# Layer 0's entry: six tiles of the first head summed side by side, between the modulation quarters

## The chip, the cores and the metric

One core of a Trainium2 chip runs the whole kernel. The metric is the device time of one execution in microseconds, here the median of several runs. In the profile PE is the matrix engine (PEld its weight loads), DVE, ACT and POOL are the vector, scalar and general-purpose engines, and SP issues most DMAs.

## What is computed

Two layers of a transformer over 512 latent tokens and 256 context tokens, D = 1024, in float32. Each layer is a mixer followed by a gated feed-forward, and each of the two reads a normalised input that is scaled and shifted by vectors made from a conditioning vector:

```python
s_c = jax.nn.silu(c)                       # (1, 1024); s_cc the same for the context
mx = (s_c @ mod_w[l] + mod_b[l])[:, None]  # 6 x 1024 numbers: shift, scale, gate, twice
shx1, scx1, gx1, shx2, scx2, gx2 = jnp.split(mx, 6, axis=-1)
hx = _rms(x, norm_mix_w[l]) * (1.0 + scx1) + shx1
qa_x, ka_x, va_x, qb_x, kb_x, vb_x = heads(hx @ w_in, True)    # layer 0
```

The change concerns only the beginning of layer 0: the first two of the six modulation parts (shift `part` 0 and scale `part` 1), the normalised and modulated input, and its product with the columns of `w_in` that belong to the first of four KV heads (256 query columns, 64 key, 64 value: 384 columns).

## The kernel before

**Tiles.** The 768 tokens are six tiles of 128: 0 to 3 latent, 4 and 5 context. `CTX_FIRST = (4, 5, 0, 1, 2, 3)` is the order in which they are worked. D is eight K-slices of 128 (`KT`). A product in float32 is done as three products of `float32r` halves: every operand is split into a high half (a cast on ACT) and a low half (a subtraction on DVE or POOL), and `project` (L460) adds high x high, high x low and low x high for each K-slice. So a tile's sum for one head is 8 x 3 = 24 products of 128 x 384.

**Modulation.** `mod_steps` (L168) makes a quarter `n` (256 columns, two K-slices of the later input) of one `part`: two loads of 512 KB (`modw`, L177), products with the padded conditioning columns (L182), a copy to SBUF (`modr`, L185), then `yield`; after it, four small products that turn the row into columns (`modcol`, L191) and `add_mod` (L276, L280), which writes the shift `modc` or the scale `aff`. The `modw` tiles and the head's weight tiles share the tag `mw` with six buffers; two more stand under the tag `raw`.

**The entry, L1149 to L1213.** Quarters 0 and 1 are started, the x tiles loaded; each x tile is squared (ACT, L1166), scaled by its inverse root (POOL L159 and L160, DVE L1167), transposed on PE (L1171) and copied to `xT` on ACT (L1172). Then quarter 2, and quarter 3 under a PE order that is written out by hand (`manual_schedule`); elsewhere a list scheduler orders each engine's instructions ahead of time, by program order and its own cost model. `modulated(k)` applies scale and shift to K-slice k of `xT` (DVE, L1184), casts the high halves (ACT, L1189) and subtracts for the low ones (L1190: POOL for the context's two tiles, DVE for the latent tiles). `weights0` (L481) loads the head's weights in four units of two K-slices (`wir`, L491) and splits them (L498, L499). The hand-written part sums only the two context tiles, and that in pieces around the end of quarter 3; their PSUM banks are halves of `inps` tiles of the score pool.

**Behind it.** `tables0` makes the rotary tables (`rw`, `rp`, `rt`, L383 to L392). `in_proj0` (L505) goes through the tiles in `CTX_FIRST` order: for each it sums what is not yet summed (`project`, in four quarters between which it yields), copies the sum out of PSUM (`qkv`, L520, two buffers), squares and reduces (L440, L442), takes the inverse root on POOL (L159, L160), rotates (`qy`, `qz`, L449 to L457, two buffers each), scales (L523) and splits into high and low halves for queries (`qd`) and keys (`kd`, the low half on POOL at L530). PE turns them (`qpt`, `kpt`) and ACT copies them out (`qt`, `kT`); with both context tiles' `kT` the first scores can start (L578). The sums of tiles 2 and 3 stand in the banks `acc0` and `acc1`. All sums of the later heads use `acc0`, so head 1 starts when tile 2 has been copied out. From then on each attention step of one head carries a tile's sums of the next.

Of the kernel before, what the change touches and what calls it, by code (L numbers as in the profile page):

```python
# [11 lines left out]
F32 = mybir.dt.float32  # L12
# [21 lines left out]
THETA = 10000.0  # L34
CTX_FIRST = (4, 5, 0, 1, 2, 3)
WBUF = 5
PBUF = 4
MODS0 = (0, 2, 2, 0)
LAM_INIT = 0.8 - 0.6 * math.exp(-0.3)
# [24 lines left out]
def backbone(es: ExitStack, tc: tile.TileContext, x, c, ctx, c_ctx, mod_w, mod_b, norm_mix_w, norm_ffn_w,  # L64
# [103 lines left out]
    def mod_steps(l, part, n, new_tile, pool, bank, wide=None, room=("modr", 1)):  # L168

        width, pieces = 256, 2  # L170
        c0 = part * D + n * width
        ps = p_1.tile([P, width], F32, name="mod", tag=bank) if wide is None else \
            wide.pool.tile([P, 1024], F32, name="mod", tag="sc", bufs=2)[:, :width]
        kp = KT // pieces
        for pc in range(pieces):
            w = new_tile([P, kp, width], "modw")
            nc.sync.dma_start(  # L177
                w, mod_w[l, pc * kp * P:(pc + 1) * kp * P, c0:c0 + width].rearrange("(j p) n -> p j n", p=P))
            for a in range(kp):
                k = pc * kp + a  # L180
                j = k % 4
                nc.tensor.matmul(ps[32 * j:32 * j + 32, :], s_pad[:, k, :], w[:, a, :],  # L182
                                 start=k < 4, stop=k >= 4, tile_position=(0, 32 * j))
        r = pool.tile([P, width], F32, name="modr", tag=room[0], bufs=room[1])
        turn["modr"] = nc.scalar.copy(r, ps)  # L185
        yield
        nb = width // P
        k0, k1 = n * nb, (n + 1) * nb
        pc2 = p_1.tile([P, nb, 2], F32, name="modcol", tag=bank)
        for b in range(nb):  # L190
            nc.tensor.matmul(pc2[:, b, :], r[:, b * P:(b + 1) * P], sel2, start=True, stop=True)  # L191
        add_mod(l, part, k0, k1, pc2, 2)
# [285 lines left out]
        return hi, lo  # L478


    def weights0(b, wp, subs, new_tile=raw_tile, loads=((0, 1), (), (2,), (3,))):  # L481

        qc, kc, vc = ((b * 256, 512 + 64 * b, 640 + 64 * b) if b < 2 else
                      (768 + (b - 2) * 256, 1280 + 64 * (b - 2), 1408 + 64 * (b - 2)))
        for u in range(4):
            if not u:
                raws = []
            for v in loads[u]:
                raws.append(new_tile([P, 2, 384], "wir"))
                for c0, c1, s in ((0, 256, qc), (256, 320, kc), (320, 384, vc)):  # L490
                    turn["load"] = nc.sync.dma_start(  # L491
                        raws[-1][:, :, c0:c1],
                        ev_w_in[0, v * 256:(v + 1) * 256, s:s + c1 - c0].rearrange("(j p) n -> p j n", p=P))
            if not u:
                yield
            raw = raws.pop(0)
            hi, lo = (wp.tile([P, 2, 384], F32R, name=f"wi{z}", tag=f"w{z}", bufs=WBUF + 1) for z in ("hi", "lo"))
            nc.scalar.copy(hi, raw)  # L498
            subs[u % len(subs)].tensor_sub(lo, raw, f32(hi))  # L499
            yield hi, lo  # L500
# [4 lines left out]
    def in_proj0(b, ws, tabs, wp, st, later, begun={}):  # L505
# [5 lines left out]
        for t in CTX_FIRST:  # L511
            ps = begun[t] if t in begun else acc_tile("inps", 384, one=int(b == 0 and t == CTX_FIRST[-1]))
            for k in range(0, KT, 2):
                if k:
                    yield
                if b == 0 and t in CTX_FIRST[:2]:
                    continue
                project(ps, t, ws, 0, 384, range(k, k + 2))
            raw = wp.tile([P, 384], F32, name="qkv", tag="qkv", bufs=2)
            nc.scalar.copy(raw, ps)  # L520
            nc.gpsimd.tensor_copy(vv[:, t, :], raw[:, 320:384])
            y, r = rotate(raw[:, 0:320], 4, 1, t, *tabs[b // 2], wp)
            nc.gpsimd.tensor_tensor(y, y, bc(r, 2, HD), ALU.mult)  # L523
            qd = wp.tile([P, 4, 2, HD], F32R, name="qd", tag="qd", bufs=2)
            nc.scalar.copy(qd[:, :, 0, :], y[:, 0:4])
            nc.vector.tensor_sub(qd[:, :, 1, :], y[:, 0:4], f32(qd[:, :, 0, :]))
            kd = wp.tile([P, 2, 2, HD], F32R, name="kd", tag="kd", bufs=2)
            kb = bc(y[:, 4, :], 1, 2)
            nc.scalar.copy(kd[:, 0], kb)
            nc.gpsimd.tensor_sub(kd[:, 1], kb, f32(kd[:, 0]))  # L530
# [616 lines left out]


    def start_tile(shape, name):  # L1149
        return start.pool.tile(shape, F32, name=name, tag="mw", bufs=6)  # L1150

    def start_mod(n):
        for part in range(2):
            mod_chunk(0, part, n, start_tile, start.pool, f"acc{part}", p_sc)

    p_sc = Pool("p_sc0", space=PSUM)
    wp = Pool("mw0", "right")
    xs = {t: load_x(t) for t in CTX_FIRST[:2]}
    start_mod(0)
    start_mod(1)  # L1160
    xs.update({t: load_x(t) for t in CTX_FIRST[2:]})
    xT = start.pool.tile([P, KT, TOK], F32, name="xT")
    for t in CTX_FIRST:
        h = start.pool.tile([P, D], F32, name="nh", tag="nh", bufs=2)
        ss = small.tile([P, 1], F32, name="nss", tag="nss")
        nc.scalar.activation(h, xs[t], AF.Square, accum_out=ss)  # L1166
# [1 line left out]
        for g in range(2):  # L1168
            pt = tr_tile("npt", [P, 4, P])
            for k in range(4):  # L1170
                nc.tensor.transpose(pt[:, k, :], h[:, (4 * g + k) * P:(4 * g + k + 1) * P], ident)  # L1171
            nc.scalar.copy(xT[:, 4 * g:4 * g + 4, t * P:(t + 1) * P], pt)  # L1172
    start_mod(2)
    late = [mod_steps(0, part, 3, (raw_tile, start_tile)[part], start.pool, f"acc{part}") for part in range(2)]
    manual = tc.manual_schedule(engines={mybir.EngineType.PE})
    manual.__enter__()
    for g in late:
        next(g)
    units = weights0(0, wp.pool, (nc.vector,), start_tile, ((0, 1, 2, 3), (), (), ()))
    next(units)  # L1180

    def modulated(k):
        for i, (s0, s1) in ((1, (SEQ, TOK)), (0, (0, SEQ))):
            nc.vector.tensor_scalar(xT[:, k, s0:s1], xT[:, k, s0:s1], aff[0][:, 0, k, i:i + 1],  # L1184
                                    modc[0][:, 0, k, i:i + 1], ALU.mult, ALU.add)
        for s0, s1, ks in ((SEQ, TOK, slice(k - 1, k + 1)), (0, SEQ, slice(k, k + 1))):
            if s0 == 0 or k % 2:
                hi, lo = (cols_T(j, s0, s1)[:, ks, :] for j in range(2))
                turn["started"] = nc.scalar.copy(hi, xT[:, ks, s0:s1])  # L1189
                (nc.gpsimd if s0 else nc.vector).tensor_sub(lo, xT[:, ks, s0:s1], f32(hi))  # L1190

    ws, begun, first = [], {}, CTX_FIRST[:2]
    for k in range(6):
        modulated(k)
        if k % 2:
            ws += islice(units, 1)
# [3 lines left out]
    for t in first:  # L1200
        project(begun[t], t, ws, 0, 384, range(2), ((0, 0), (1, 0)))
        if t == first[0]:
            for g in late:
                for _ in g:
                    pass
    for t in first:
        project(begun[t], t, ws, 0, 384, range(2), ((0, 1),))
    for k in range(6, KT):
        modulated(k)
    ws += units  # L1210
    for k in range(2, KT, 2):
        for t in first:
            project(begun[t], t, ws, 0, 384, range(k, k + 2))  # L1213
    manual.__exit__(None, None, None)

    mods = [(0, part, n) for part in (2, 3, 4) for n in range(4)]
    tabs = {}
    tables0(0, tabs, wp.pool)

    start.close()  # L1220
    at = Pool("mix0")
    sink = at.pool.tile([P, 8], F32, name="sink")
    nc.sync.dma_start(sink, dram_rows(ev_sink_a[0]))
# [63 lines left out]
    next(units)  # L1287
    with behind("started"):
        ws = [next(units) for _ in range(2)]
    if True:  # L1290
# [640 lines left out]
```

## Time and profile before

| | us |
|---|---|
| median of 3 runs | 1695.58 |
| lowest and highest run | 1693.07, 1696.42 |
| span of the profiled execution | 1695.6 |
| PE busy | 1631.5 (96%) |
| DVE, ACT, POOL busy | 1146.7, 937.0, 696.4 |

A timeline row is: start, duration, engine, line, operation, tile written and tiles read, sizes, and in brackets how long the engine was idle before and what ended that. Rows that follow one another and are alike are merged; their count stands behind "x". Starts are microseconds from the span's start. The modelled ends of products overlap, so the time of one is read from start to start.

### The profile page before, as it was taken

The page shows a single profiled execution, that of the slowest core. Times are in us where ns is not written, and L with a number is a line of the kernel's source. Part 1 is how long each engine was busy: PE and PEld are TensorE (multiplying, and loading weights), DVE is VectorE, ACT ScalarE, POOL GpSimd, SP SyncE. Part 2 cuts the span into 40 slices and gives each one's busy share as a digit, 9 for nine tenths or more (in the row PEclk, how much of TensorE's full clock was granted, in tenths as well). Part 3 has the DMA queues.
Part 4 walks back from the last instruction along what each step waited for, and adds up shares of the span by engine and source line. Part 5 has one row for each costly group of instructions (what it writes and reads, how often), then busy time and mean ns, then how long its engine had stood idle before and what let it go on. Part 6 is the DMA issues. An engine that isn't in the chain of part 4 may idle for free. (4 is left out here: it accounts for less than half of the span.)

```text
span 1695.6 us, 28585 instructions
## 1 busy us (share of the span) xinstructions
PE 1631.5 (96%) x10390; PEld 1468.6 (87%) x10390; DVE 1146.7 (68%) x2014; ACT 937.0 (55%) x2011; POOL 696.4 (41%) x867
## 2 busy tenths in 40 slices
PE   6999999899999999999999989999999999999998
PEld 3977787677999999998777889999988899999887
DVE  3765656754799887767767656666666598887434
ACT  5565555745456665545554456666666555555320
POOL 2665554321346554412413366666664242221000
PEclk8999999999999999999999999999999999999999
DMA  9222221411455555439966311111112433331431
GB/s 319 69 71 74 70 70 50 164 60 38 129 167 172 164 159 162 134 108 347 296 184 189 99 43 38 48 42 44 50 45 97 125 93 102 111 101 57 137 99 62
DMA packets 218108, 194.64 MB, mean 115 GB/s; under 512 B 20016, under 2 KB 202864, under 8 KB 217968
## 3 DMA queue, kind: packets, MB, share of 16 engines
q1 hardware_dynamic: 217616, 192.62, 36.8%
q8 instruction: 81, 1.33, 0.3%
q14 instruction: 59, 0.48, 0.1%
q10 hardware_dynamic: 352, 0.21, 0.0%
HBM read 179.92 MB, written 12.87 MB: 114 GB/s over the span
## 5 line engine op out<-in xcount | busy, mean ns | idle before, releaser
L901 ACT CAST wbh<-wr 128x512 fp32r<-128x512 f32 x170 | 104.9, 621 | 130.2 <-PE p L933 73.4
L933 PE MATMUL p<-hT,wbh 128*128 128x256 f32 (+1 forms) x752 | 154.5, 299 | 0.0
L465 PE MATMUL inps<-wih,hT 128*128 128x384 f32 x512 | 144.2, 344 | 7.3 <-ACT qkv L677 7.3
L911 POOL TENSOR_TENSOR wbl<-wr,wbh 128x512 fp32r<-128x512 f32 x43 | 60.0, 1396 | 173.6 <-ACT wbh L901 173.6
L933 PEld LDWEIGHTS p<-hT,wbh 128*128 128x128 f32 x752 | 121.9, 191 | 0.2
L911 DVE TENSOR_TENSOR wbl<-wr,wbh 128x512 fp32r<-128x512 f32 x127 | 107.7, 858 | 21.0 <-ACT wbh L901 16.8
L933 PE MATMUL p<-hT,wbl 128*128 128x256 f32 (+1 forms) x376 | 111.9, 298 | 0.0
L933 PE MATMUL p<-t,wbh 128*128 128x384 f32 (+1 forms) x480 | 111.3, 318 | 0.0
L604 POOL TENSOR_SCALAR Pt<-Pt,rc 128x256 f32<-128x256 f32 (+3 forms) x96 | 74.6, 788 | 89.3 <-DVE rc L601 83.1
L231 POOL TENSOR_TENSOR modp<-modp 128x512 f32<-128x512 f32 x40 | 57.4, 1436 | 114.3 <-ACT modp L230 114.3
L465 PEld LDWEIGHTS inps<-wih,hT 128*128 128x128 f32 x512 | 93.3, 188 | 10.6 <-ACT qkv L677 9.7
L933 PE MATMUL p<-hTt,wbh 128*128 128x256 f32 (+1 forms) x480 | 101.0, 302 | 0.0
L887 POOL TENSOR_TENSOR wr<-wr 128x512 f32<-128x512 f32 x40 | 61.6, 1540 | 89.8 <-DVE ws L892 85.8
L933 PE MATMUL p<-b,wbh 128*128 128x384 f32 x368 | 93.8, 336 | 0.2 <-DVE c L961 0.2
L901 ACT CAST wbh<-ws 128x512 fp32r<-128x512 f32 x120 | 69.4, 579 | 43.1 <-PE p L933 29.0
L224 DVE SCALAR_TENSOR_TENSOR ma<-modw,cols,ma 128x256 f32<-128x256 f32 x140 | 89.2, 637 | 2.3
L592 ACT ACTIVATE Pt<-sc,nm 128x256 f32<-128x256 f32 (+3 forms) x96 | 67.6, 707 | 35.3 <-DVE nm L588 16.9
L465 PE MATMUL inps<-wil,hT 128*128 128x384 f32 x256 | 86.0, 336 | 0.0
L933 PEld LDWEIGHTS p<-t,wbh 128*128 128x128 f32 x480 | 82.9, 189 | 0.0
L911 DVE TENSOR_TENSOR wbl<-ws,wbh 128x512 fp32r<-128x512 f32 x120 | 81.7, 681 | 1.7 <-ACT wbh L901 1.6
L933 PEld LDWEIGHTS p<-hTt,wbh 128*128 128x128 f32 x480 | 78.3, 191 | 3.1 <-ACT modp L230 1.6
L230 ACT ACTIVATE modp<-modw,cols 128x256 f32<-128x256 f32 x160 | 68.4, 500 | 18.0 <-POOL ma L236 10.1
(355 smaller groups left out, 5217.9 us busy)
## 6 DMA issues: line engine op xcount, KB each, us to landing
modw<-in_mod_w_dram SPq DMA_DIRECT2D x96, 512.0 KB, 5.2
wr<-in_ffn_w_in_dram SPq DMA_DIRECT2D x176, 256.0 KB, 2.9
wdr<-in_ffn_w_out_dram SPq DMA_DIRECT2D x66, 512.0 KB, 3.7
wir<-in_od_w_in_dram SPq DMA_DIRECT2D x96, 128.0 KB, 2.3
hidm<-hid SPq DMA_DIRECT2D x44, 192.0 KB, 1.9
hr<-hidm SPq DMA_DIRECT2D x22, 192.0 KB, 3.5
x<-in_x_dram SPq DMA_DIRECT2D x8, 512.0 KB, 3.5
wir<-in_ev_w_in_dram SPq DMA_DIRECT2D x16, 256.0 KB, 3.5
```

Source lines behind the costliest of these rows:

```text
L224: nc.vector.scalar_tensor_tensor(acc, w[:, k], scale[k], acc, ALU.mult, ALU.add)
L230: nc.scalar.activation(pr[:, k], w[:, k], AF.Copy, scale=scale[k])
L231: nc.gpsimd.tensor_add(pr[:, 0:2], pr[:, 0:2], pr[:, 2:4])
L465: nc.tensor.matmul(ps, hs[j][:, k, :], ws[k // 2][z][:, k % 2, c0:c1], start=(k, j, z) == (0, 0, 0), stop=(k, j, z) == (KT - 1, 1, 0))
L592: turn["exp"] = nc.scalar.activation(p[:, :n], s, AF.Exp, bias=nm[:, c1], accum_out=sm[:, c1])
L604: nc.gpsimd.tensor_scalar(p[:, :n], p[:, :n], rc[:, hh:hh + 1], 1.0, ALU.mult, ALU.mult)
L887: nc.gpsimd.tensor_sub(w, raw[f, "G1"], w)
L901: nc.scalar.copy(hi, w)
L911: (nc.gpsimd if name == "G2" else nc.vector).tensor_sub(lo, raw[need[n]], f32(hi))
L933: nc.tensor.matmul(ps, w[:, k, :], H[b][h][:, k, :], start=first and k == 0 and q == 0, stop=final and k == 3 and q == 2, skip_group_check ...
```

## The change

- `MW = 7`: seven `mw` buffers. Quarter 0 stands in the banks `acc0` and `acc1`, the later ones in `tr0` and `tr1`; `modr` has two buffers; part 1 of quarters 2 and 3 is loaded into the two `raw` buffers.
- The hand-written PE order begins before the first product and covers the whole entry. It reads: quarter 0's products, the context tiles' transposes, quarter 0's column products, the latent tiles' transposes, K-pair 0 of the context tiles; then for n = 1, 2, 3: products of quarter n, K-pair n-1 of tiles 0 and 1, column products of n, K-pair n-1 of tiles 2 and 3, K-pair n of the context tiles (for n = 3 of all six tiles).
- A weight unit is loaded behind each quarter, one at a time (`apart`).
- DVE takes the second half of the copies to `xT`; context and latent halves of a K-pair are modulated one after the other.
- All six sums are done when `in_proj0` begins, which leaves them out. Sink and head 1's weights are issued on SP behind the last `modw`; the rotary tables' DVE steps stand behind the last low half, and each weight unit's DVE split behind the low halves of the quarter before.

```diff
@@ weights0
-            if not u:
+            if not u or apart:
                 yield
@@ in_proj0
-                if b == 0 and t in CTX_FIRST[:2]:
+                if t in begun:
                     continue
@@ entry
-    start_mod(0)
-    start_mod(1)
...
+    def chunk_rows(n):
+        chunks[n] = [mod_steps(0, part, n, raw_tile if n > 1 and part else start_tile, start.pool, f"{'tr' if n else 'acc'}{part}", room=("modr", 2))
+                     for part in range(2)]
+        for g in chunks[n]:
+            next(g)
+
+    def chunk_columns(n):
+        for g in chunks.pop(n):
+            for _ in g:
+                pass
...
-            nc.scalar.copy(xT[:, 4 * g:4 * g + 4, t * P:(t + 1) * P], pt)
+            (nc.vector.tensor_copy if g else nc.scalar.copy)(xT[:, 4 * g:4 * g + 4, t * P:(t + 1) * P], pt)
+
+    def modulated(n, i):
+        s0, s1 = ((0, SEQ), (SEQ, TOK))[i]
+        ks = range(2 * n, 2 * n + 2)
+        for k in ks:
             nc.vector.tensor_scalar(xT[:, k, s0:s1], xT[:, k, s0:s1], aff[0][:, 0, k, i:i + 1],
                                     modc[0][:, 0, k, i:i + 1], ALU.mult, ALU.add)
+        for kk in [slice(ks[0], ks[0] + 2)] if i else [slice(k, k + 1) for k in ks]:
+            hi, lo = (cols_T(j, s0, s1)[:, kk, :] for j in range(2))
+            turn["started"] = nc.scalar.copy(hi, xT[:, kk, s0:s1])
+            turn["lows"] = (nc.gpsimd if i else nc.vector).tensor_sub(lo, xT[:, kk, s0:s1], f32(hi))
+
+    def begin(n, *tiles):
+        for t in tiles:
+            project(begun[t], t, ws, 0, 384, range(2 * n, 2 * n + 2))
+
+    chunk_rows(0)
+    units = weights0(0, wp.pool, (nc.vector,), start_tile, ((0,), (1,), (2,), (3,)), True)
+    next(units)
+    xs.update({t: load_x(t) for t in CTX_FIRST[2:]})
+    for t in CTX_FIRST[:2]:
+        turned_x(t)
+    chunk_columns(0)
+    modulated(0, 1)
+    ws.append(next(units))
+    for t in CTX_FIRST[2:]:
+        turned_x(t)
...
+    for i, t in enumerate(CTX_FIRST[4:]):
+        begun[t] = acc_tile("inps", 384, one=i)
+    modulated(0, 0)
+    begin(0, *CTX_FIRST[:2])
+    for n in range(1, 4):
+        chunk_rows(n)
+        next(units)
+        begin(n - 1, *CTX_FIRST[2:4])
+        chunk_columns(n)
+        with behind("lows"):
+            ws.append(next(units))
+        for i in (1, 0):
+            modulated(n, i)
+        begin(n - 1, *CTX_FIRST[4:])
+        begin(n, *CTX_FIRST[:2 if n < 3 else NT])
...
+    last_modw = turn["modw"].ins
+    with behind("lows"):
+        tables0(0, tabs, wp.pool)
...
+    with tc.issue_after(last_modw):
+        nc.sync.dma_start(sink, dram_rows(ev_sink_a[0]))
...
     units = weights0(1, wp.pool, (nc.gpsimd, nc.vector))
-    next(units)
+    with tc.issue_after(last_modw):
+        next(units)
```

More of the change, by code (lines that the diff above doesn't have):

```diff
@@ L36 @@
 WBUF = 5
+MW = 7
 PBUF = 4
@@ L176, in mod_steps @@
             w = new_tile([P, kp, width], "modw")
-            nc.sync.dma_start(
+            turn["modw"] = nc.sync.dma_start(
                 w, mod_w[l, pc * kp * P:(pc + 1) * kp * P, c0:c0 + width].rearrange("(j p) n -> p j n", p=P))
@@ L478, in split, with weights0 @@
         return hi, lo
-    def weights0(b, wp, subs, new_tile=raw_tile, loads=((0, 1), (), (2,), (3,))):
+    def weights0(b, wp, subs, new_tile=raw_tile, loads=((0, 1), (), (2,), (3,)), apart=False):
         qc, kc, vc = ((b * 256, 512 + 64 * b, 640 + 64 * b) if b < 2 else
@@ L1149, in start_tile @@
     def start_tile(shape, name):
[L1150 to L1154, printed above, removed]
+        return start.pool.tile(shape, F32, name=name, tag="mw", bufs=MW)
     p_sc = Pool("p_sc0", space=PSUM)
@@ L1158, in backbone, with turned_x @@
     xs = {t: load_x(t) for t in CTX_FIRST[:2]}
-    start_mod(0)
-    start_mod(1)
-    xs.update({t: load_x(t) for t in CTX_FIRST[2:]})
     xT = start.pool.tile([P, KT, TOK], F32, name="xT")
-    for t in CTX_FIRST:
+    manual = tc.manual_schedule(engines={mybir.EngineType.PE})
+    manual.__enter__()
+    chunks, ws, begun = {}, [], {}
+    def chunk_rows(n):
[7 more added lines that the diff above has]
+                pass
+    def turned_x(t):
         h = start.pool.tile([P, D], F32, name="nh", tag="nh", bufs=2)
@@ L1171, in backbone @@
                 nc.tensor.transpose(pt[:, k, :], h[:, (4 * g + k) * P:(4 * g + k + 1) * P], ident)
-            nc.scalar.copy(xT[:, 4 * g:4 * g + 4, t * P:(t + 1) * P], pt)
[L1173 to L1179, printed above, removed]
-    next(units)
-    def modulated(k):
-        for i, (s0, s1) in ((1, (SEQ, TOK)), (0, (0, SEQ))):
+            (nc.vector.tensor_copy if g else nc.scalar.copy)(xT[:, 4 * g:4 * g + 4, t * P:(t + 1) * P], pt)
[3 more added lines that the diff above has]
+        for k in ks:
             nc.vector.tensor_scalar(xT[:, k, s0:s1], xT[:, k, s0:s1], aff[0][:, 0, k, i:i + 1],
                                     modc[0][:, 0, k, i:i + 1], ALU.mult, ALU.add)
[L1186 to L1196, printed above, removed]
+        for kk in [slice(ks[0], ks[0] + 2)] if i else [slice(k, k + 1) for k in ks]:
[16 more added lines that the diff above has]
+        turned_x(t)
     for i in range(0, 4, 2):
@@ L1199, in backbone @@
         begun[CTX_FIRST[i]], begun[CTX_FIRST[i + 1]] = sc[:, :384], sc[:, 512:896]
[L1200 to L1213, printed above, removed]
+    for i, t in enumerate(CTX_FIRST[4:]):
[13 more added lines that the diff above has]
+        begin(n, *CTX_FIRST[:2 if n < 3 else NT])
     manual.__exit__(None, None, None)
@@ L1217, in backbone @@
     tabs = {}
-    tables0(0, tabs, wp.pool)
+    last_modw = turn["modw"].ins
+    with behind("lows"):
+        tables0(0, tabs, wp.pool)
     start.close()
@@ L1222, in backbone @@
     sink = at.pool.tile([P, 8], F32, name="sink")
-    nc.sync.dma_start(sink, dram_rows(ev_sink_a[0]))
+    with tc.issue_after(last_modw):
+        nc.sync.dma_start(sink, dram_rows(ev_sink_a[0]))
     negsink = at.pool.tile([P, 8], F32, name="negsink")
@@ L1286, in backbone @@
     units = weights0(1, wp.pool, (nc.gpsimd, nc.vector))
-    next(units)
+    with tc.issue_after(last_modw):
+        next(units)
     with behind("started"):
```

## The prediction

> **What bounds the kernel now.** I read the page first, then busy time by windows over the entry, then each engine's timeline there.
>
> ```profile
> span 1695.6 us, 28585 instructions
> ...
> PE   6999999899999999999999989999999999999998
> ...
> DMA  9222221411455555439966311111112433331431
> ```
>
> ```profile
> 20.00:30.00 10.00, 8.60 (x46) 6.31 (x47) 4.71 (x10) 6.33 (x14) 3.48 (x7) 0.52 1.10 347
> 30.00:40.00 10.00, 6.45 (x65) 3.56 (x64) 6.39 (x13) 4.77 (x10) 1.86 (x1) 0.84 1.07 311
> ```
>
> ```profile
> 80.00:180.00 100.00, 93.46 (x711) 75.75 (x710) 62.41 (x189) 62.44 (x182) 61.09 (x104) 1.00 0.24 71
> ```
>
> The window rows give start and end, length, the busy time of PE, PEld, DVE, ACT and POOL with instruction counts, granted clock, DMA share and GB/s. PE is above 90% nearly everywhere; only the first of the 40 slices (42 us each) is low, and there DMA is full at 311 to 347 GB/s. So the kernel is PE work behind a load-bound entry. The change can win only in that entry; behind it, with PE 93% busy from 80 to 180, an earlier start passes on about one for one. The span is 1695.6 us and the median of the runs 1695.58, so I sum against the span and add nothing.
>
> ```profile
> 62.36 0.34 PE L465 MATMUL inps<-wilo,hT 128*128 128x384 f32 x1
> ...
> 62.88 0.34 PE L465 MATMUL inps<-wilo,hT 128*128 128x384 f32 x1
> ...
> 69.84 0.39 PE L465 MATMUL inps<-wihi,hT 128*128 128x384 f32 x1
> 70.45 0.44 PE L465 MATMUL inps<-wihi,hTc 128*128 128x384 f32 x1 [0.23 <-ACT qkv L520]
> ...
> 77.39 0.70 PE L578 MATMUL sc<-kT,qt 128*128 128x256 f32 x4
> ```
>
> ```profile
> 58.40 0.86 ACT L520 COPY qkv<-inps 128x384 f32<-128x384 f32 x2 [3.57 <-PE inps L465]
> ...
> 65.23 0.29 ACT L529 CAST kd<-qy 128x128 fp32r<-128x128 f32 x1
> ...
> 69.92 0.48 ACT L520 COPY qkv<-inps 128x384 f32<-128x384 f32 x1 [1.33 <-DVE qy L456]
> 70.30 0.47 ACT L440 ACTIVATE sq<-qkv 128x320 f32<-128x320 f32 x1
> ```
>
> ```profile
> 61.48 2.32 POOL L160 TENSOR_TENSOR rs_q<-rs_q,neghalf 128x5 f32<-128x5 f32 x2
> 63.88 0.20 POOL L159 TENSOR_SCALAR rs_q<-qss 128x5 f32<-128x5 f32 x1
> 64.16 1.41 POOL L523 TENSOR_TENSOR qy<-qy,rs_q 128x320 f32<-128x320 f32 x2
> ...
> 66.84 0.49 POOL L530 TENSOR_TENSOR kd<-qy,kd 128x128 fp32r<-128x128 f32 x1
> 67.31 1.84 POOL L499 TENSOR_TENSOR wilo<-wir,wihi 128x768 fp32r<-128x768 f32 x1
> ```
>
> ```profile
> 67.37 2.46 DVE L456 TENSOR_TENSOR qy<-qkv,rt 128x256 f32<-128x256 f32 x2 [0.35 <-POOL kd L530]
> ```
>
> Read this as two clocks side by side. PE: the first head's sums run to 70.23 (the first score follows at 77.39); one product to the next takes 0.52/3 = 0.173 us (62.36 to 62.88 spans three), so six tiles x 24 products are 25.0 us. Rotations: the first copies out of PSUM are at 58.40; tile 4's last step, `kd`, ends at 67.33, 8.9 us on; only then is a `qy` buffer (of two) free for the third tile (67.37), and only when that tile is read is a `qkv` buffer free for the fifth (69.92). The copy at 69.92 frees bank `acc0` and head 1's sums start, 0.23 us after PE was ready. **At 70 us, sums and rotations are late together**: making the sums alone earlier is worth little.
>
> **The change, part by part.** *Moved:* 96 products of four tiles (the two context tiles were already begun) from behind the loads to between them, 96 x 0.173 = 16.6 us of PE; three quarters of all 144 could now stand under loads. Do they fit?
>
> ```profile
> 2.10 6.30 SPq L177 DMA_DIRECT2D modw<-in_mod_w_dram  x6
> ...
> 14.85 1.07 PE L182 MATMUL mod<-modw,s_pad 128*32 128x256 f32 x16
> ...
> 17.36 1.06 ACT L1166 ACTIVATE nh<-x 128x1024 f32<-128x1024 f32 x1 [1.37 <-DMA x<-in_x_dram]
> ...
> 20.36 1.94 PE L1171 MATMUL npt<-cst,nh 128*128 128x128 f32 x8 [2.74 <-DVE modc L276]
> ...
> 44.30 0.50 PE L191 MATMUL modcol<-cst,modr 128*128 128x2 f32 x4
> ```
>
> *Start of the sums.* In PE's written order they stand behind the transposes of all six tiles. The first latent tile landed at 17.36 behind six 512 KB pieces; now four pieces and one weight tile (384 KB) are ahead. At 347 GB/s a piece is 1.5 us, the weight tile 1.1: 17.36 - 3.0 + 1.1 = 15.5, the fourth tile 4.5 later. A tile takes 3.0 us from its square to its transposes (17.36 to 20.36) and 1.1 to 1.9 there; with two `nh` buffers the third waits for the first. At 1.5 each they end at 20.0, 21.5, 24.5, 26.0: **sums from about 26.0**.
>
> *Work from there on PE.* 25.0 of sums, six groups of 16 modulation products at about 1.0 (row 14.85) and six of four column products at 0.4 to 0.5 (row 44.30), 2.2 in all with the overlap: 33.2 us. The last loads land near 41 (12.5 MB in pieces of the sizes above, 13.5 million bytes with the small ones, at 347 GB/s from 2.1), so **PE, not DMA, now ends the entry**.
>
> *Clock.*
>
> ```profile
> 38.00:40.00 2.00, 2.00 (x17) 0.73 (x18) 0.00 (x0) 0.00 (x0) 0.00 (x0) 0.50 0.88 214
> ...
> 42.00:44.00 2.00, 2.00 (x15) 1.19 (x8) 2.00 (x5) 1.87 (x4) 0.00 (x0) 0.50 0.87 285
> 44.00:46.00 2.00, 2.00 (x14) 2.00 (x14) 2.00 (x5) 2.00 (x5) 1.92 (x1) 0.94 0.29 73
> ```
>
> The granted clock is 0.50 while PE works between waits, and returns soon after 44, some 6.2 us into nearly unbroken work from 38. Around 26 the same mix of transposes and waits is ahead, so I take half clock for 6.2 us: 3.1 us lost (bounds 0, and 5.0 from the ten us of 20 to 30 at 0.52). The Trainium skill, "TensorE: Matmul & The Clock Gate", Part 1, has half clock set in only after an idle window of about 3.4 us. The one idle time in row 20.36, 2.74 us, was enough here, so this trace does not bear it out.
>
> *The wait that is added.* Each round, `begin(n, ctx)` needs the context's low halves, and everything in PE's queue stands behind it.
>
> ```profile
> 39.77 1.02 PE L191 MATMUL modcol<-cst,modr 128*128 128x2 f32 x4
> ...
> 41.22 1.65 DVE L1184 TENSOR_SCALAR xT<-xT,aff,modc 128x256 f32<-128x256 f32 x4
> ...
> 42.13 0.62 ACT L1189 CAST hT<-xT 128x512 fp32r<-128x512 f32 x1
> ```
>
> ```profile
> 24.84 1.27 POOL L1190 TENSOR_TENSOR hTc<-xT,hTc 128x512 fp32r<-128x512 f32 x1
> ...
> 35.37 1.86 POOL L1190 TENSOR_TENSOR hTc<-xT,hTc 128x512 fp32r<-128x512 f32 x1 [7.97 <-ACT hTc L1189]
> 44.08 2.89 POOL L1190 TENSOR_TENSOR hTc<-xT,hTc 128x512 fp32r<-128x512 f32 x1 [6.85 <-ACT hTc L1189]
> ```
>
> From the column products' end (40.79) the pieces start to be scaled 0.43 later, two context pieces take about 0.8, the cast 0.62, POOL 1.27 to 2.89; I take 1.86, as DVE works beside it: 3.9 us with hand-overs. Twelve products of two latent tiles (2.07) and two with high halves (0.35) cover 2.4: a stall of 1.5, three times, 4.5 us (bounds 0.7 and 2.5 each).
>
> *Sum.* 26.0 + 33.2 + 3.1 + 4.5 = 66.8: the sums end 3.4 us before 70.23. But with every tile's last pair in the final round, the first tile is ready at 66.8 - 5 x 1.04 = 61.6, **3.2 us later than 58.40**. What is late next is the rotation. Tile 4 now comes a microsecond ahead of tile 5, not together with it and a third. Its chain from the rows above: copy 0.48, square 0.47 and reduction about as much, POOL's root 0.20 + 1.16, scaling 0.70, cast 0.29 and `kd` 0.49 are 4.3; with one root step of the next tile (1.16) between, 5.5 in place of 8.9. These are the ends; I take 5.5, since the third tile is no longer in POOL's queue. `kd` then ends at 67.1 against 67.33, and the next tile gains a further 1.3 as the 1.84 us subtraction at 67.31 moves off its way. Together about **1.5 us gained: 1694.1**.
>
> *At nothing:* the seventh `mw` buffer; DVE taking half of the xT copies (DVE is 4.7 of 10 busy there); twelve weight DMAs now between the modulation loads on SP (the bytes are the same, and SP issued six pieces in 6.30 us whose transfer took 9). The last quarter sits in the two `raw` buffers, so the rope table and head 1's first weight tiles are loaded behind its products, near 54; they are needed near 70. If that cover goes, one load and split is 3 to 4 us. The tables' DVE steps wait behind the last low halves; tile 4 needs only the weight row.
>
> **Rivals.** *Full clock and short stalls* (0.22). If PE stays at full clock from 26 and POOL takes 1.27: 3.1 + 3 x 0.6 = 4.9 earlier, 1689.2. For it: dense products are what brought the clock back at 44. Against it: 0.52 for ten microseconds with PE 86% busy.
>
> *No half clock, stalls as forecast* (0.04): 3.1 earlier, 1691.0. That is what the page's rule on the clock would give.
>
> *The rotations start later and run as before* (0.22), the slower side. If the rotation keeps its 8.9 us, the 3.2 us of the later first copy go straight through; with half clock for ten microseconds 1.9 more: 1695.6 + 5.1 = 1700.7. It decides from a first copy at 61.8 on. For it: POOL's order is fixed ahead of time, and tile 4 had 8.9 us in it where 4.3 do. Against it: three tiles queued there together, which is gone. The Trainium skill, "SBUF — State Buffer", section "SBUF: two separate sides", has DVE and GpSimd exclude each other on a shared port pair; 1.27 against 2.89 us for one subtraction agrees, and at 2.89 three times the sum would be 3.1 us higher, 1697.2.
>
> *Loads set the end* (0.02). Sums done 10 us behind the last load, near 51, and rotations 16 us earlier: 1679. Against it: 33.2 us of PE work do not fit between 26 and 51.
>
> **How the numbers follow.** The forecast has 0.50, with an own range of 1690.5 to 1698.5 from the bounds of clock and stalls. A measurement here tells about 0.2% (3.4 us) from no change. Of the forecast's 0.50, 0.08 lies below 1692.2 and 0.02 above 1699. Faster: 0.08 + 0.22 + 0.04 + 0.02 = 0.36; slower: 0.22 + 0.02 = 0.24; the rest, 0.40, within. The range 1687 to 1700.5 leaves out the far case and some of the slower one.
>
> **What would show it.** In the changed profile: latent transposes done near 26; clock 0.50 there and 1.00 from 32; three stalls of PE at L465 on POOL's `hTc`, 11 us apart; the first `qkv` copy near 61.6 and the last first-head product near 66.8; PE idle for two or three microseconds until the fifth `qkv` copy near 69; the first score at 74 to 77. I am wrong if the first copy comes before 58 (faster), if first copy and first score both move out by three or more (slower), or if a difference arises after 180 us, where nothing was changed.

## The result and the profile after

The changed kernel takes **1708.97 us** (median of 4 runs, 1703.14 to 1711.97) against 1694.7 beside it: ratio 1.0076, 95% interval 1.0057 to 1.0095. It is slower, above the upper end of the range (1700.5).

Two rows of the page after: the span, 12.9 us longer, and PE's busy share in 40 slices.

```profile
span 1708.5 us, 28586 instructions
...
PE   6789999899999999999999989999999999999998
```

The first slice (43 us) holds the same 6; the second fell from 9 to 7 and the third from 9 to 8. The time is lost behind the loads, where the kernel was full. PE's timeline after, over the entry:

```profile
26.34 1.94 PE L1180 MATMUL npt<-cst,nh 128*128 128x128 f32 x8 [0.40 <-DVE nh L1176]
...
50.06 0.62 PE L466 MATMUL inps<-wihi,hTc 128*128 128x384 f32 x2 [0.73 <-POOL hTc L1192]
...
66.09 0.34 PE L466 MATMUL inps<-wihi,hT 128*128 128x384 f32 x1
71.47 0.37 PE L544 MATMUL kpt<-identr,kd 128*128 128x128 f32 x1 [5.04 <-ACT kd L530]
...
78.43 0.65 PE L466 MATMUL inps<-wihi,hTc 128*128 128x384 f32 x1
...
84.36 0.71 PE L579 MATMUL sc<-kT,qt 128*128 128x256 f32 x4
```

The sums do what they were meant to do: they end at 66.43 instead of 70.23. But head 1's products start at 78.43 instead of 70.45 and the first score at 84.36 instead of 77.39. Between 66.43 and 78.43 PE has five short groups of transposes. The windows of 4 us show this hole (columns as in the prediction), and that the clock falls in it, in the trace from 70.6 on for 10.2 us:

```profile
66.00:70.00 4.00, 0.43 (x3) 0.11 (x1) 1.56 (x5) 1.64 (x4) 3.69 (x7) 1.00 0.66 187
70.00:74.00 4.00, 0.67 (x4) 0.52 (x4) 3.52 (x5) 1.42 (x4) 3.55 (x6) 0.58 0.41 102
74.00:78.00 4.00, 1.03 (x7) 0.66 (x5) 2.19 (x5) 2.56 (x6) 3.41 (x4) 0.50 0.46 130
78.00:82.00 4.00, 4.00 (x18) 4.00 (x19) 2.94 (x9) 2.30 (x7) 3.50 (x6) 0.64 0.39 129
```

To weigh this, cut both traces at three marks: the first copy of a sum out of PSUM (`qkv`), the first output of attention (the first copy `o<-av`), and the last one of layer 0. Before, by windows:

```profile
0.00:58.40 58.40, 42.15 (x291) 31.26 (x292) 28.93 (x56) 30.36 (x57) 15.00 (x23) 0.85 0.80 252
58.40:93.97 35.57, 33.75 (x220) 30.28 (x219) 24.52 (x70) 23.02 (x66) 28.86 (x50) 1.00 0.22 66
93.97:396.37 302.40, 283.10 (x2018) 225.58 (x2017) 184.70 (x403) 176.41 (x429) 135.59 (x204) 0.99 0.24 77
```

After, by windows at the same marks:

```profile
0.00:62.31 62.31, 47.14 (x332) 36.78 (x333) 29.14 (x56) 26.91 (x50) 12.53 (x23) 0.95 0.72 228
62.31:101.88 39.57, 28.48 (x183) 25.19 (x182) 28.54 (x80) 24.34 (x67) 30.95 (x52) 0.87 0.26 74
101.88:407.88 306.00, 286.88 (x2013) 227.28 (x2014) 185.39 (x402) 176.96 (x428) 133.51 (x203) 0.98 0.24 76
```

Length minus PE's busy time is PE's idle time (ends of products are modelled, so it is good to some tenths). Up to the first output PE is busy 75.9 us before (42.15 + 33.75) and 75.6 after, for nearly as many instructions (511 and 515). It is idle 18.1 us before and 26.3 after. **The first output's 7.9 us are idle time of PE, and they arise between the marks: 1.8 us idle there before, 11.1 after.** Before the first copy PE even idles 1.1 us less. Of the other 5.0 us of the span, 3.6 arise within attention, where PE's idle time is the same (19.3 and 19.1) and its busy time 3.8 us longer, with 10.2 us at half clock in the trace against 3.4; 1.4 us arise behind it. All that arises in attention is there at the third output, on ACT's timeline first before, then after:

```profile
123.21 0.37 ACT L625 COPY o<-av 128x256 f32<-128x256 f32 x1 [2.08 <-PE av L623]
```

```profile
135.16 0.37 ACT L626 COPY o<-av 128x256 f32<-128x256 f32 x1 [0.18 <-PE av L624]
```

The changed kernel is 11.9 us behind here, and 11.5 at the last output of layer 0.

### The profile page after: what moved, and what is told of

The parts are those of the page before. It is cut to its first block, busy times and chain, and to the rows that moved or that the text cites. A ratio compares the mean times of both kernels' runs of the same rounds, so it can differ in the third digit from the quotient of the medians.

```text
span 1708.5 us, 28586 instructions
## 1 busy us (share of the span) xinstructions
PE 1634.1 (96%) x10390; PEld 1469.5 (86%) x10390; DVE 1147.8 (67%) x2020; ACT 935.6 (55%) x2005; POOL 695.8 (41%) x867
## 5 line engine op out<-in xcount | busy, mean ns | idle before, releaser
L888 POOL TENSOR_TENSOR wr<-wr 128x512 f32<-128x512 f32 x40 | 61.6, 1541 | 84.3 <-DVE ws L893 82.8
```

The lines of the kernel that those rows point to most:

```text
L888: nc.gpsimd.tensor_sub(w, raw[f, "G1"], w)
```

## The experiments

At first three causes for the late rotations were on the table. **A**: quarter 3 holds the two `raw` buffers, so the rope table and head 1's weights come late and collide with the rotations. **B**: the tables' DVE steps, behind the last low halves, hold the first rotation up. **C**: the two `qy` buffers, with six sums ready together. The rotations' own rows after, first DVE's timeline:

```profile
61.29 1.84 DVE L388 TENSOR_SCALAR rw<-rw 128x64 f32<-128x64 f32 x1
63.05 0.49 DVE L391 TENSOR_TENSOR rt<-rp,rw 128x256 f32<-128x256 f32 x1
...
64.58 1.02 DVE L450 TENSOR_TENSOR qy<-qkv,rw 128x256 f32<-128x256 f32 x4
```

and POOL's timeline:

```profile
60.68 2.40 POOL L500 TENSOR_TENSOR wilo<-wir,wihi 128x768 fp32r<-128x768 f32 x1 [0.47 <-ACT wihi L499]
...
70.99 1.81 POOL L500 TENSOR_TENSOR wilo<-wir,wihi 128x768 fp32r<-128x768 f32 x1 [0.20 <-ACT wihi L499]
72.88 0.25 POOL L160 TENSOR_SCALAR rs_q<-qss 128x5 f32<-128x5 f32 x1
73.22 0.65 POOL L531 TENSOR_TENSOR kd<-qy,kd 128x128 fp32r<-128x128 f32 x1
```

and ACT's timeline, with the first and the fifth copy out of PSUM:

```profile
62.31 0.86 ACT L521 COPY qkv<-inps 128x384 f32<-128x384 f32 x2 [1.71 <-PE inps L466]
...
68.92 0.83 ACT L499 CAST wihi<-wir 128x768 fp32r<-128x768 f32 x1 [2.36 <-DMA wir<-in_ev_w_in_dram]
...
77.53 0.48 ACT L521 COPY qkv<-inps 128x384 f32<-128x384 f32 x1 [0.98 <-DVE qy L457]
```

The first rotation step waits for the tables until 64.58; a weight subtraction of head 1 stands in POOL's queue ahead of tile 4's `kd`, which ends at 73.87; the fifth copy comes 15.2 us behind the first (11.5 before).

This table has all runs (us; copy and output are the two marks; idle is PE's, between the marks and from the start to the first output; "attention" is the first to the last output; the kernel before beside these runs had medians of 1694.5 to 1694.8). Medians and ratios are of 4 to 12 runs, which for one kernel lie up to 9.3 us apart (e10); the marks and idle times are of one profiled execution each:

| kernel | median | ratio (95%) | copy | output | idle between | idle to output | attention |
|---|---|---|---|---|---|---|---|
| before | 1695.58 | | 58.40 | 93.97 | 1.8 | 18.1 | 302.4 |
| after | 1708.97 | 1.0076 (1.0057–1.0095) | 62.31 | 101.88 | 11.1 | 26.3 | 306.0 |
| e1 | 1714.81 | 1.0122 (1.0105–1.0139) | 68.31 | 105.75 | 8.3 | 26.3 | 304.7 |
| e2 | 1713.24 | 1.0111 (1.0096–1.0126) | 67.01 | 106.51 | 10.3 | 30.4 | 303.0 |
| e3 | 1700.45 | 1.0038 (1.0025–1.0051) | 62.66 | 100.17 | 8.3 | 23.7 | 298.6 |
| e4 | 1710.62 | 1.0094 (1.0077–1.0112) | 68.57 | 105.86 | 7.0 | 25.5 | 304.9 |
| e5 (on before) | 1696.35 | 1.0012 (0.9999–1.0025) | 58.01 | 92.57 | 1.4 | 17.0 | 303.6 |
| e6 | 1705.65 | 1.0069 (1.0054–1.0084) | 62.49 | 100.25 | 6.9 | 21.2 | 302.5 |
| e7 | 1703.63 | 1.0053 (1.0033–1.0073) | 66.86 | 103.14 | 9.0 | 26.2 | 299.5 |
| e8 | 1705.42 | 1.0068 (1.0053–1.0083) | 66.09 | 102.46 | 7.1 | 23.6 | 303.1 |
| e9 | 1703.01 | 1.0053 (1.0032–1.0074) | 59.02 | 97.11 | 9.7 | 23.5 | 302.8 |
| e10 | 1700.16 | 1.0024 (1.0009–1.0039) | 59.09 | 96.50 | 6.2 | 19.1 | 299.5 |
| e11 (on before) | 1696.59 | 1.0010 (1.0000–1.0021) | 56.69 | 91.38 | 1.3 | 16.0 | 305.6 |
| e12 | 1701.62 | 1.0041 (1.0026–1.0057) | 62.00 | 102.17 | 8.1 | 22.8 | 298.2 |
| e13 | 1695.40 | 1.0002 (0.9991–1.0012) | 56.78 | 92.33 | 2.6 | 18.3 | 301.3 |
| e14 | 1703.69 | 1.0054 (1.0041–1.0067) | 58.72 | 99.20 | 1.3 | 20.9 | 301.3 |
| e15 | 1703.17 | 1.0056 (1.0042–1.0069) | 64.45 | 103.39 | 4.3 | 22.9 | 300.6 |
| e16 | 1695.83 | 1.0003 (0.9993–1.0014) | 56.53 | 89.34 | 0.4 | 16.0 | 305.5 |

### Tables, raw buffers, and the ring of two (e1 to e6)

**e1**: tables early, and quarter 3 out of the raw buffers.

```diff
-        ... mod_steps(0, part, n, raw_tile if n > 1 and part else start_tile, ...
+        ... mod_steps(0, part, n, start_tile, ...
-    with behind("lows"):
-        tables0(0, tabs, wp.pool)
+    tables0(0, tabs, wp.pool)
```

> The changed kernel, but with the rotary tables' DVE steps no longer held behind the last low halves, and with all modulation quarters in the mw buffers, so that the two raw buffers are free for the rope table and head 1's weights. In the changed kernel SP issues nothing between 55.9 and 64.6 us, head 1's products start at 78.4 and the first score at 84.4. Theory A (the raw buffers: head 1's weights land in the middle of the rotations) and theory B (the table steps on DVE delay the first rotation, 64.6 instead of 62.9): both causes are gone, head 1 starts near 71 to 73, the time falls by 5 to 8 us, to 1701 to 1704. Theory C (six sums that end together, 4 us later than before, and a rotation chain with two buffers that is slow by itself): head 1 still starts after 76 and the time falls by less than 3 us.

**e2**: tables late as in the change, quarter 3 out of the raw buffers, the rope table in an `mw` buffer.

```diff
-        rp = raw_tile([P, NTX, 2, HD], "rp")
+        rp = new_tile([P, NTX, 2, HD], "rp")   # start_tile for head 0
-        ... mod_steps(0, part, n, raw_tile if n > 1 and part else start_tile, ...
+        ... mod_steps(0, part, n, start_tile, ...
```

> The same, but the table steps stay behind the last low halves, and the rope table has an mw buffer of its own, so that it holds up no load. Only A's cause is gone. A: most of e1's gain, first qy still near 64.5, head 1 from 73 to 74, 3 to 5 us faster than the changed kernel. B: at most 1 to 2 us. C: none.

**e3**: tables early, the rope table in an `mw` buffer, quarter 3 left in the raw buffers.

> The table steps are free and the rope table stands in an mw buffer, but quarters 2 and 3 keep the raw buffers, so head 1's first two weight units load behind the products of quarter 3 (about 54 us) and the others behind those. B's cause is gone, A's half: A predicts a gain between that of e2 and none, B nearly e1's time, with the first qy at 62.9.

**e4** is e1, **e5** the kernel before, **e6** e3, each with a third `qy` buffer (room for it from `grow`, which has one buffer less).

```diff
-        y = pool.tile([P, n, HD], F32, name="qy", tag="qy", bufs=2)
+        y = pool.tile([P, n, HD], F32, name="qy", tag="qy", bufs=3)
```

> e1 with three qy buffers in place of two (paid for with one grow buffer less). C predicts that the third tile's qy comes some 6 us earlier, right behind its copy, that head 1 starts at 70 or before and that the time falls by 3 to 6 us below e1. A and B predict within 1.5 us of e1.

> The kernel before with three qy buffers (one grow buffer less), nothing else. In it the first copy is at 58.4, the fifth at 69.9 and PE has no idle time until 70.2. Theory R (the rotations bind only where the sums are already done; in the kernel before the fourth and fifth sums end at 68 to 70 anyway): within 3 us of before. Rival (the two qy buffers bind the kernel before as well): 3 to 5 us faster than before.

> The run with early tables and the raw buffers kept (1700.5, fifth copy 12.5 us behind the first, head 1's products from 75.7) with three qy buffers. Theory R: the fifth copy comes 7 us behind the first, at 69 to 70, head 1 starts there, PE's hole between 66.3 and head 1 shrinks from 9 to 3 or 4 us, and the time falls by 4 to 6 us, to 1695 to 1697. Rival (the hole is made by head 1's late weights, not by the rotations): head 1 starts where its second pair of weights allows, after 73, and the time stays above 1698.

e1 and e2 came out slower, which was not expected: without the raw buffers, quarter 3's loads wait for an `mw` buffer. SP's timeline of e1, in which four pieces of the modulation take 13.44 us to issue (11.69 in e2), and in which the second half of head 1's weights is issued behind the first copy:

```profile
33.80 13.44 SPq L178 DMA_DIRECT2D modw<-in_mod_w_dram  x4
...
69.91 2.93 SPq L492 DMA_DIRECT2D wir<-in_ev_w_in_dram  x6
```

So the first copy moves out by 6.0 and 4.7 us, and their times say nothing about the rotations; the length between the marks does. It is 39.5 us in e2, as after (39.6), although half of head 1's weights are loaded ahead of the first copy in e2, a quarter of them after: **this part of A is worth nothing.** The other half is still issued behind the first copy (67.79 us in e2, 69.91 in e1), and in e1 ACT waits 2.15 us for it, much as after (2.36); what that costs was not tried. The length is 37.4 in e1 and 37.5 in e3, with the tables early: **B holds, and is worth 2.1 us between the marks.** In e3 the scale of the weight row, 1.84 us behind the low halves, takes 0.20, on DVE's timeline:

```profile
32.67 0.20 DVE L388 TENSOR_SCALAR rw<-rw 128x64 f32<-128x64 f32 x1 [0.65 <-DMA rw<-in_ev_qn_a_dram]
```

e3's first output is only 1.7 us earlier than after's, but its median is 8.5 us lower; in the traces attention is 7.4 us shorter (298.6 us instead of 306.0, none of it at half clock), and most of that is there at the third output, 126.73 instead of 135.16.

**C**: the third buffer brings the fifth copy to 7.2 us behind the first in e6 (12.5 in e3), and head 1's products to 70.16 (75.71). The first output does not move: 100.25 against 100.17. Of e6 by windows:

```profile
78.00:82.00 4.00, 1.86 (x8) 1.52 (x9) 2.96 (x7) 1.92 (x6) 3.83 (x7) 0.92 0.00 0
```

PE started head 1 earlier and ran dry later, from 78 on, while POOL has no gap. The hole moved: in e6 the third buffer does not bring the first output forward. Its times don't settle more. e4 is 4.2 us faster than e1, as C had it, e6 is 5.2 us slower than e3, where 4 to 6 us faster was expected, and e5 takes the time of the kernel before. But all three gave up a `grow` buffer for it, and where two `grow` copies follow one another, the second now waits for the first to be written out. PE's timeline of e5:

```profile
220.49 1.94 PE L612 MATMUL ppt<-cst,Pt 128*128 128x128 f32 x8 [3.56 <-DVE grow L290]
```

In the kernel before this wait is 0.31 us. From the ninth output to the last of layer 0 the kernels with three `qy` buffers (e4, e5, e6, e8) take 210.4 to 211.7 us, all others 205.7 to 207.9. So these four runs time two edits at once: in e5 the third output is 3.8 us earlier than before (119.46 us), and the median has nothing of it left. What a third `qy` buffer alone is worth stays open.

### Four tiles (e7, e8)

**e7** is e3 with only four tiles in the written rounds; **e8** adds the third `qy` buffer.

```diff
-    for i, t in enumerate(CTX_FIRST[4:]):
-        begun[t] = acc_tile("inps", 384, one=i)
...
-        begin(n - 1, *CTX_FIRST[2:4])
+        begin(n - 1, CTX_FIRST[2])
...
-        begin(n - 1, *CTX_FIRST[4:])
-        begin(n, *CTX_FIRST[:2 if n < 3 else NT])
+        begin(n - 1, CTX_FIRST[3])
+        begin(n, *CTX_FIRST[:2 if n < 3 else 4])
```

> Early tables, raw buffers kept, two qy buffers, but only four tiles (context, 0 and 1) are summed between the quarters; tiles 2 and 3 are summed whole behind them, as in the kernel before. Theory R (six sums that end together leave PE nothing to do while the rotations run): the first copy comes 2 to 4 us earlier, at 58 to 60, tiles 2 and 3 (8.3 us of products) stand in the hole, sums end near 70, head 1 starts at 71 to 73, the time is 1695 to 1698. Rival (what matters is how much is summed under the loads): 4 us or more slower than with six, above 1704.

> Both: four tiles and three qy buffers. Theory R: the fifth sum, not the rotation, comes last again, head 1 starts at 70 to 71 and the time is 1692 to 1696, the best of the changed kernels. Rival as for the four tiles: above 1700.

The edit did not do what was meant. The list scheduler put the last two tiles' products between the rounds all the same, each group behind a wait of its own; PE's timeline of e7:

```profile
41.54 0.62 PE L466 MATMUL inps<-wihi,hT 128*128 128x384 f32 x2 [0.48 <-DVE hT L1193]
...
52.66 0.62 PE L466 MATMUL inps<-wihi,hT 128*128 128x384 f32 x2 [0.48 <-DVE hT L1193]
```

The first copy is 4.2 us later than in e3, and neither run answers the question.

### An earlier first copy, and a lighter POOL (e9 to e12)

**e9** is e3 with the modulation products one quarter further ahead. Two theories: the time follows the first copy (**S**), or POOL, busy 31.3 of the 37.5 us between the marks in e3, sets the pace. **e10** is e9, **e11** the kernel before and **e12** e3 with two of POOL's jobs given to DVE.

```diff
@@ e9
+    chunk_rows(1)
     for n in range(1, 4):
-        chunk_rows(n)
         next(units)
         begin(n - 1, *CTX_FIRST[2:4])
         chunk_columns(n)
+        if n < 3:
+            chunk_rows(n + 1)
@@ e10, e11, e12
-            nc.gpsimd.tensor_sub(kd[:, 1], kb, f32(kd[:, 0]))
+            (nc.gpsimd if b else nc.vector).tensor_sub(kd[:, 1], kb, f32(kd[:, 0]))
-    units = weights0(1, wp.pool, (nc.gpsimd, nc.vector))
+    units = weights0(1, wp.pool, (nc.vector,))
```

> Early tables, raw buffers kept, all six tiles, but the products of quarter n+1 stand right behind the column products of n, where PE otherwise waits for the context's low halves. Theory S (in all changed kernels the first attention output comes 36 to 40 us behind the first copy, whatever else differs: 39.5 with late tables, 37.4 with early ones, 35.6 in the kernel before; the stretch is that of the rotations, mostly on POOL, and the time follows the first copy): the three stalls of 1.1 us and some more go, the first copy comes near 59 in place of 62.7, the first output near 96.3, and the time is 1695 to 1698. Rival (PE's hole behind the sums is what costs): the sums end earlier too, the hole stays 9 us, the time falls by less than 2 us from 1700.5.

> The same, and for the first head the key's low halves, as well as head 1's weight splits, are on DVE instead of POOL: 6 x 0.49 + 2 x 2.0 us of POOL's 31 us between first copy and first output are gone. Theory S with POOL as the bound: the stretch is 3 to 5 us shorter and the time as much lower than e9. Rival (the chain of one tile with its hand-overs binds, not POOL's sum): within 1.5 us of e9.

> The kernel before with the same two moves from POOL to DVE. POOL as the bound from 58.4 to 94: first output 2 to 4 us earlier, 1691 to 1693. Rival: within 1.5 us of before.

> Early tables and raw buffers kept (1700.5; first copy 62.7, first output 37.5 behind it) with the two moves from POOL to DVE. POOL as the bound: the output 33 to 35 us behind the first copy, 1696 to 1698. Rival: 36.5 or more, above 1699.

e9's marks fell as expected (59.02 and 97.11), its time did not: 1703.01, no better than e3's 1700.45. S holds up to the first output at most; the rival had it that the hole stays at 9 us and the time doesn't follow, and the idle time between the marks is 9.7. Relieving POOL did not shorten the way between the marks: 37.4 us in e10 against 38.1 in e9, and 40.2 in e12 against 37.5 in e3; in e11 it is 34.7 against 35.6, with the time as before. (e10's median is 2.9 us below e9's, between the two expectations.) By windows between the marks, e10:

```profile
59.09:96.50 37.41, 31.25 (x192) 27.54 (x191) 28.05 (x86) 24.59 (x70) 28.08 (x47) 0.86 0.24 73
```

POOL is down from 32.0 us in e9 to 28.1, PE still idle for 6.2, and the clock 0.86 there. So in these kernels POOL's load alone isn't what sets the end. What is common to all changed kernels so far is PE's idle time behind the sums, and what none of them had is work for PE there.

### Work held back for the hole (e13 to e16)

The question that was left: is PE idle because its products now all stand *ahead* of the rotations (**K**), or do the rotations pace everything whatever PE has to do (**R**)? **e13** is e9 with the edit of e7 and, this time, the last two tiles' 48 products held back in PE's queue behind the rounds. **e14** holds back four tiles. **e15** is the changed kernel with this edit alone; **e16** is e13 with e10's lighter POOL.

```diff
-                project(ps, t, ws, 0, 384, range(k, k + 2))
+                with behind("begun"):
+                    project(ps, t, ws, 0, 384, range(k, k + 2))
...
     manual.__exit__(None, None, None)
+    turn["begun"] = turn["prod"]     # the last product of the rounds
```

> As e9 (tables early, modulation products one quarter further ahead), with the last two of the six tiles left out of the side-by-side rounds and their 48 products (0.17 us each, 8.2 us) held back in PE's order behind the rounds, where PE was idle in e9 for 9.7 us between the first copy and the first output. K (the hole is PE's missing work): that idle time falls to 2 to 4 us, the first copy comes 0 to 4 us before e9's 59.0, the first output at 89 to 94 instead of 97.1, and the run takes 1692 to 1697 us. R (the rotations pace it): the idle time stays with 8 to 10 us counted from the program's start to the first output, the first output stays within 1.5 us of 97.1, and the run takes 1701 to 1704.

> As e13 with four tiles' products (96, 16.3 us) held back: only the first two tiles are summed in the rounds. K: PE is idle 1 to 3 us between the first copy and the first output, as in the kernel before (1.8), which comes 34 to 37 us behind the first copy, at 90 to 95; the run takes 1692 to 1697. R: the first output at 96 to 98, the run 1701 to 1704.

> The changed kernel with only this edit: the last two tiles' 48 products out of the rounds and held back behind them; tables and modulation as in the change. K: PE's idle time between the first copy and the first output falls from 11.1 to 3 to 6 us, the first output comes at 95 to 98 instead of 101.9, the run takes 1700 to 1705. R: the first output stays at 100 to 102.5, the run at 1706 to 1711.

> e13 with POOL relieved as in e10 (head 0's key differences and head 1's weight differences on DVE). K: where PE has work beside the rotations, POOL's load does not set the end, so the first output is within 1 us of e13's and the run within 2 us of e13's. R: the first output 1 to 3 us before e13's, the run 1 to 3 us faster.

**e13 met K at every point.** By windows between the marks, first e9, then e13:

```profile
59.02:97.11 38.09, 28.41 (x183) 25.27 (x182) 27.95 (x75) 23.38 (x67) 32.04 (x52) 0.91 0.22 67
```

```profile
56.78:92.33 35.55, 32.96 (x220) 30.13 (x218) 26.81 (x73) 23.29 (x66) 30.81 (x51) 1.00 0.25 73
```

37 more PE instructions lie between the marks, POOL and DVE have about as much to do, PE's idle time falls from 9.7 to 2.6 us, and the clock there is 1.00 throughout. The first output comes 4.8 us earlier, and the time is 7.6 us lower: that of the kernel before. e15 shows the same edit alone on the changed kernel: idle 4.3 instead of 11.1, time 5.8 us lower. Its first output was expected at 95 to 98 and came at 103.39: with two tiles' products gone, PE runs dry inside the rounds, as its timeline shows,

```profile
38.76 0.69 PE L466 MATMUL inps<-wihi,hTc 128*128 128x384 f32 x1 [2.86 <-ACT hTc L1192]
40.12 1.01 PE L466 MATMUL inps<-wihi,hTc 128*128 128x384 f32 x2 [0.35 <-POOL hTc L1193]
```

and the first copy comes 2.1 us later, with 17.1 us at half clock up to there in the trace (6.8 in the changed kernel). In e13 the next quarter's modulation products stand in the rounds as well, and 6.8 us are at half clock. e14 goes too far the same way: hardly idle between the marks (1.3 us), but short of work in the rounds. By windows of 4 us, e14:

```profile
40.00:44.00 4.00, 2.47 (x34) 0.93 (x35) 3.78 (x11) 2.29 (x5) 1.80 (x1) 1.00 0.74 237
44.00:48.00 4.00, 1.69 (x6) 1.37 (x7) 1.60 (x3) 0.37 (x1) 2.73 (x1) 0.64 0.62 170
48.00:52.00 4.00, 3.85 (x16) 3.76 (x14) 0.28 (x2) 0.00 (x0) 0.00 (x0) 0.50 0.10 19
52.00:56.00 4.00, 1.90 (x5) 1.39 (x6) 3.64 (x8) 2.95 (x5) 1.80 (x2) 0.50 0.00 0
```

It met K's idle time, and neither K's first output nor K's time; its time, 1703.69, is within what R had. e16 is split: its first output is 3.0 us before e13's, as R had it, its time e13's within 0.4 us, as K had it; its attention takes 4.2 us longer (PE is busy 4.0 us longer in it), so the earlier output was not kept.

The first output was too early a mark for e15 and e16. By the third one e15 is 5.2 us ahead of the changed kernel (130.00 us against 135.16, PE idle for 7.1 us less up to there), e13 7.9 us ahead of e9 (121.28 against 129.22, 5.7 us less), and e16 with 122.03 behind e13: close to the differences of the medians, 5.8, 7.6 and 0.4. So what holding the products back is worth in time is there at the third output, mostly as idle time of PE that is gone. No version was faster than the kernel before.

## Why the prediction was wrong

- **The way to the end of the sums: right in kind, its end in part by luck.** The last product was to be done at 66.8 and was at 66.43, the first copy was to come at 61.6 and came at 62.31. But the latent transposes were to end at 26.0 and ended at 28.28, 2.3 us late, and the three stalls on POOL's `hTc` were to cost 1.5 us each and show 0.73 each, 2.3 us less together. Half clock was to last 6.2 us from about 26 on; it lasted 3.4 us twice, from 19.4 and from 26.2 on, and only the second reaches into the sums.
- **The step that failed: "What is late next is the rotation ... 5.5 in place of 8.9."** From the first copy to the end of tile 4's `kd` it took 11.6 us (62.31 to 73.87). The 4.3 us of the chain were single durations with every queue empty, and the queues were not: the tables' steps, head 1's weight subtraction and the next tiles' roots stand among them. The fifth copy, forecast near 69, came at 77.53, and PE's hole, forecast at two or three microseconds, is 12.0 us long. The forecast had 1.5 us gained, the traces have 12.9 lost. Of these 14.4 us, 0.7 lie in the first copy, 8.7 between it and the first output (4.0 longer, where the forecast had 3.4 and 1.3 less) and 5.0 behind.
- **"The tables' DVE steps wait behind the last low halves; tile 4 needs only the weight row": costed at nothing, worth 2.1 us between the marks** (e1 against e2, e3 against after). The weight row itself is the first of these steps, and it took 1.84 us, not the 0.20 of the kernel before.
- **"The 1.84 us subtraction moves off its way" was wrong**: it runs at 70.99, 1.81 us long, ahead of `kd`. The loads "needed near 70" kept ACT waiting for 2.36 us until 68.92. Neither is shown to have cost the end much: with half of the weights early (e2) the way between the marks is as long, and with the subtraction on DVE it is 0.7 us shorter (e10 against e9) or 2.7 longer (e12 against e3).
- **What the working lacked altogether** is the other half of the sentence "sums and rotations are late together". Before, 58.4 to 70.2 was PE's time with tiles 0 to 3's sums *while* tiles 4 and 5 were rotated. Moving these products ahead of the loads' end takes the cover off the rotations. e13 puts a third of the products back and has the time of before, with tables and modulation as in e9.
- **The slower rival had the right side and place**: "the rotations start later and run as before", from a first copy at 61.8 on. Its price, 5.1 us, was too low: the first copy is 3.9 us later, not 3.2, the way from it to the first output 4.0 us longer, not equal, and 5.0 us come behind that.
- **An earlier or later start passes on "about one for one": not at once.** The lag is 7.9 us at the first output and 11.9 at the third. Between the two, PE waits on attention's own steps and half clock comes with it, from 121.8 us on for 6.8; PE's timeline after:

```profile
123.24 1.44 PE L579 MATMUL sc<-kT,qt 128*128 128x256 f32 x4 [1.69 <-ACT Pt L593]
```

e15 has no such wait between these two outputs and no half clock. Why one kernel has them and the other not is open: nothing was tried that sets them alone. From the third output on the lag stays between 11.5 and 14.3 us and ends at 12.9: of "a difference after 180 us" there is about 1 us in the end.

## What to carry to other kernels

Before you move an engine's work into an early gap, look up what that work covers where it stands: if a chain on other engines runs beside it, the gap moves behind the chain and comes back with its hand-overs. Fill the early gap with part of the work and hold the rest back in the queue, and check in the trace that the scheduler did hold it back. A chain that is moved is priced by walking each engine's queue at its new place, with the steps that you meant to cost at nothing. And an experiment that pays for one buffer with another changes two things: look in its trace where the other one was used.

## What the runs showed of the hardware

Half clock comes in blocks: in all these traces a stretch of 0.50 lasts about 3.4, 6.8, 10.2 or 13.7 us, but for one cut off by the end. It sets in after idle time of PE: in the 3.4 us ahead of each block of the first 400 us, PE was idle for 0.8 us or more. It costs a quarter to a half of its length in attention: PE is busy there for 281.8 to 282.8 us where the trace has no half clock (e3, e7, e12, e14), for 286.8 to 287.0 with 10.2 us of it (after, e11, e16) and for 285.6 with 13.7 (e4). The Trainium skill, "TensorE: Matmul & The Clock Gate", Part 1, has a free-running window of 3413 ns, half clock after an idle one and full clock after a busy one. The blocks agree with the window, and the hole agrees with the idle one (no product from 66.43 to 71.47, half clock from 70.6). e14 agrees with neither: its half clock begins at 45.1, behind 3.4 us in which PE is busy for 1.83, and lasts 13.7, through four us in which it is busy for 3.85 (row 48.00:52.00).

One and the same small step on DVE took 0.20 us alone (e3) and 1.84 us while POOL subtracted 128x768 beside it (60.68 to 63.08; 1.83 in e2 in the same place); the forecast had weighed such sharing for POOL's subtraction only.
